# Rank scatter through a Pool ring: ring of four groups, direct rows in pairs of tiles, and an extra Pool drain

## Chip, cores, metric

One core of one Trainium2 chip. The metric is the device time of one execution in microseconds (us); medians of several executions are compared. The kernels of one job ran on one chip; the jobs ran on different chips (8, 1, 9 and 1), so runs of different jobs are compared by their ratio to the kernel before, which ran in every job.

## The reference

```
x: 8 x 2048 x 2560 float32, scores: 8 x 2048
ranks = argsort(argsort(scores, axis=1), axis=1)
out[b, ranks[b, n], :] = x[b, n, :]
```

Every row of 10 KB is moved to the place that its score's rank gives it: 168 MB read and 168 MB written.

## The kernel before

VectorE counts for every score how many others are smaller, which gives the rank. The rows are moved in two ways. Most go through SBUF: Pool loads a group (two tiles of 128 rows, 2.6 MB) into one of eight buffers and later scatters it with two indirect transfers. The rows of a few tiles ("direct") go from HBM to HBM, one transfer for each row, cut in 16 pieces of 640 B, issued by SyncE and ScalarE.

```
GROUPS = [(0, 1, range(B)), (P, 1, range(3))] + [(256 * i, 2, ()) for i in range(1, 8)]
#         (first row, tiles in the group, batches in which it goes direct)
ORDER = [2, 0, 1, 3, 4, 5, 6, 7, 8]
BULK = [(b, g) for b in range(B) for g in ORDER if b not in GROUPS[g][2]]
NBUF = 8
LAG = 2
...
with tc.tile_critical(no_gpsimd_drain=True):
    ...
    # SyncE and ScalarE in turn, for each direct row:
    line.eng.dma_start(
        out=out_bytes[bass.ds(at[i], ROW)], in_=x_bytes[b, row, :],
    ).then_inc(s_rows[line], 16)
    ...
    for k in range(1, NBUF):                      # Pool
        load(pl, k, s_load[k])
    for k, (b, g) in enumerate(BULK):
        i = k % NBUF
        if k >= LAG and k + NBUF - LAG < len(BULK):
            scatters_done(pl, k - LAG)            # wait: the group LAG back has landed
            load(pl, k + NBUF - LAG, s_load[(k - LAG) % NBUF])
        ...                                       # wait for load k and for the ranks
        for j in range(GROUPS[g][1]):
            scatter(k, j, 0, P, rank_i, s_scat[i][j])
    for k in range(max(0, len(BULK) - NBUF), len(BULK)):
        scatters_done(sp, k)                      # SyncE: the last waits
```

Pool's transfers run first in, first out on 16 DMA engines ("Pool's ring" below; in the profile before, all 177 landed in the order in which they were issued). A transfer has landed when its semaphore has its 16 increments. Pool's drain is an instruction at which, as e13 to e15 show, Pool waits until its transfers have landed; what more it costs is a subject of this study. LAG is how many groups may be scattered and not yet landed. With 11 direct tiles there are 61 groups, five of them of one tile ("half groups").

## Time and profile before

| | before |
|---|---|
| median of the runs | 794.83 us (794.64 to 796.62) |
| span of the profiled run | 795.4 us |
| transfers issued by Pool | 60 loads, 117 scatters |
| last scatter landed / last direct row landed | 791.3 / 727.6 us |
| Pool's drain at the very end | 3.02 us, from 791.64 |

The profiled execution was one of the slower ones (797.09 us of device time): the span is 1.6 to 2.1 us below the device time in all runs, so a run of the median should have its last landing near 789 us (an estimate). What bounds the kernel, and the lines that show it, are in the prediction.

### The profile page before, as it was taken

The page shows a single profiled execution, that of the slowest core. Times are in us where ns is not written, and L with a number is a line of the kernel's source. Part 1 is how long each engine was busy: PE and PEld are TensorE (multiplying, and loading weights), DVE is VectorE, ACT ScalarE, POOL GpSimd, SP SyncE. Part 2 cuts the span into 40 slices and gives each one's busy share as a digit, 9 for nine tenths or more (in the row PEclk, how much of TensorE's full clock was granted, in tenths as well). Part 3 has the DMA queues.
Part 4 walks back from the last instruction along what each step waited for, and adds up shares of the span by engine and source line. Part 5 has one row for each costly group of instructions (what it writes and reads, how often), then busy time and mean ns, then how long its engine had stood idle before and what let it go on. Part 6 is the DMA issues. An engine that isn't in the chain of part 4 may idle for free.

```text
span 795.4 us, 4586 instructions
## 1 busy us (share of the span) xinstructions
PE 33.3 (4%) x155; PEld 27.2 (3%) x155; DVE 411.2 (52%) x1002; POOL 148.4 (19%) x186
## 2 busy tenths in 40 slices
PE   3002010020020100200000000000000000000000
PEld 3001010010010100100000000000000000000000
DVE  6999999999999999999994000000000000000000
POOL 3102121212121212022111212122121212111600
PEclk9555555555555555555555555555555555555555
DMA  8999999999999999999999999999999999999994
GB/s 364 431 402 365 424 415 425 417 422 417 425 417 418 347 420 422 422 367 420 421 420 423 397 397 421 420 419 380 420 411 423 420 386 407 401 431 426 390 428 193
DMA packets 70737, 321.57 MB, mean 404 GB/s; under 512 B 25384, under 2 KB 47912, under 8 KB 47912
## 3 DMA queue, kind: packets, MB, share of 16 engines
q0 software_dynamic: 25488, 304.10, 91.3%
q1 hardware_dynamic: 22688, 9.94, 4.9%
q10 hardware_dynamic: 22528, 7.25, 3.9%
q14 instruction: 32, 0.26, 0.1%
q8 instruction: 1, 0.02, 0.0%
HBM read 167.84 MB, written 167.77 MB: 422 GB/s over the span
## 4 chain that ended last, share of the span: by engine, by line
DVE 47%; DMA 40%; issue 4%; POOL 3%; PE 1%; POOLq 0%; SPq 0%
DVE trash L258 41%; DMA out_dram<-x,rank_i 38%; DVE s_all L235 2%; DMA x<-in_x_dram 2%; POOL out_dram L361 2%; DVE rank L284 1%; DVE rank L290 1%; DVE rank_i L307 1%; POOL x L122 1%; DMA s_in<-in_scores_dram 0%; PE ps_all L190 0%; PE ps_col L169 0%; DVE rows_i L220 0%; POOLq L28 0%; DVE s_col L177 0%
## 5 line engine op out<-in xcount | busy, mean ns | idle before, releaser
L258 DVE TENSOR_SCALAR_CACHE_REDUCE trash<-s_all,s_col 128x1792 bf16<-128x1792 f32 (+9 forms) x248 | 315.3, 1306 | 0.3
L122 POOL DMA_DIRECT2D x<-in_x_dram x60 | 33.8, 565 | 545.8 <-DMA out_dram<-x,rank_i 376.5
L361 POOL DMA_INDIRECT out_dram<-x,rank_i x117 | 112.8, 964 | 59.0 <-issue 35.3
L258 DVE SCALAR_TENSOR_TENSOR trash<-s_all,s_col,mask 128x256 bf16<-128x256 f32 (+1 forms) x128 | 59.0, 461 | 0.0
L190 PE MATMUL ps_all<-ident,s_col 128*128 128x128 f32 x128 | 27.2, 399 | 247.4 <-DVE s_all L235 247.0
L190 PEld LDWEIGHTS ps_all<-ident,s_col 128*128 128x128 f32 x128 | 24.4, 213 | 249.4 <-DVE s_all L235 249.0
L235 DVE COPY s_all<-ps_all 128x512 f32<-128x512 f32 x32 | 20.1, 683 | 1.8 <-PE ps_all L190 1.5
L258 DVE DVE_READ_ACCUMULATOR trash<-s_all,s_col 128x1 f32 x248 | 19.9, 80 | 0.0
L290 DVE TENSOR_TENSOR rank<-rank,acc 128x2 f32<-128x2 f32 (+1 forms) x72 | 11.5, 160 | 2.5
L284 DVE TENSOR_TENSOR rank<-acc,acc 128x2 f32<-128x2 f32 (+1 forms) x72 | 11.5, 160 | 2.5
L307 DVE CAST rank_i<-rank 128x2 int32<-128x2 f32 (+1 forms) x61 | 10.7, 176 | 1.8
L258 DVE DVE_READ_ACCUMULATOR trash<-s_all,s_col,mask 128x1 f32 x128 | 10.2, 80 | 0.0
L300 PE MATMUL ps_row<-ident,rank 128*1 128x128 f32 x11 | 4.1, 372 | 101.3 <-DVE rank L290 92.7
L300 PEld LDWEIGHTS ps_row<-ident,rank 128*1 128x1 f32 x11 | 0.9, 79 | 105.0 <-DVE rank L290 95.5
L220 DVE TENSOR_SCALAR rows_i<-ps_row 1x128 int32<-1x128 f32 x11 | 3.0, 272 | 0.0
L177 DVE COPY s_col<-ps_col 128x128 f32<-128x128 f32 x1 | 0.3, 292 | 4.8 <-PE ps_col L169 4.8
L169 PE MATMUL ps_col<-ident,s_in 8*128 8x8 f32 x16 | 2.0, 261 | 4.0 <-DMA s_in<-in_scores_dram 4.0
L169 PEld LDWEIGHTS ps_col<-ident,s_in 8*128 8x128 f32 x16 | 1.9, 211 | 4.0 <-DMA s_in<-in_scores_dram 4.0
L150 POOL TENSOR_SCALAR_AFFINE_SELECT mask<-mask 128x256 f32<-128x256 f32 x2 | 0.8, 398 | 0.0
L162 DVE MEMSET acc<- 128x128 f32 x1 | 0.2, 165 | 1.1 <-SPq L98 1.1
L133 POOL MEMSET mask<- 128x512 f32 x1 | 0.5, 525 | 0.0
L132 POOL MEMSET ident<- 128x128 f32 x1 | 0.2, 204 | 0.5 <-SPq L98 0.5
(5 smaller groups left out, 0.7 us busy)
## 6 DMA issues: line engine op xcount, KB each, us to landing
x<-in_x_dram POOLq DMA_DIRECT2D x55, 2560.0 KB, 19.2
out_dram<-in_x_dram SPq DMA_DIRECT2D x704, 10.0 KB
out_dram<-in_x_dram ACTq DMA_DIRECT2D x704, 10.0 KB
x<-in_x_dram POOLq DMA_DIRECT2D x5, 1280.0 KB, 16.7
x<-in_x_dram SPq DMA_DIRECT2D x1, 2560.0 KB, 13.4
out_dram<-x,rank_i POOLq DMA_INDIRECT x117, 23.5
s_in<-in_scores_dram SPq DMA_DIRECT2D x1, 64.0 KB
```

Source lines behind the costliest of these rows:

```text
L122: line.eng.dma_start(out=xb[k % NBUF][:, :m * D], in_=x[b, r:r + P * m, :].rearrange("(p j) d -> p (j d)", j=m),).then_inc(sem, 16)
L150: nc.gpsimd.affine_select(out=part, in_=part, pattern=[[0, MMAX], [-1, P]], compare_op=OP.is_ge, fill=0.0, base=-half, channel_multiplier=1,)
L169: nc.tensor.transpose(out=ps_col[:, B * c:B * (c + 1)], in_=s_in[:, r + j:r + m * P:m], identity=ident[:B, :B],)
L190: nc.tensor.transpose(out=ps_all[:, P * c:P * (c + 1)], in_=s_col[:, c, b:b + 1].to_broadcast([P, P]), identity=ident[:],)
L220: nc.vector.tensor_scalar(out=rows_i[DIRECT.index((b, g))][:m, :], in0=ps_row[:m, :P], scalar1=float(b * N), scalar2=float(ROW), op0=OP.ad ...
L235: nc.vector.tensor_copy(out=s_all[:, 512 * q:512 * (q + 1)], in_=ps_all[:, 512 * q:512 * (q + 1)],)
L258: how.pop("do")(out=trash[i][:, :P * (hi_c - lo_c)], in0=s_all[:, P * lo_c:P * hi_c], accum_out=acc[which][:, col:col + 1], **how,)
L284: nc.vector.tensor_tensor(out=rank[:, cols], in0=acc[0][:, cols], in1=acc[1][:, cols], op=OP.add)
L290: nc.vector.tensor_tensor(out=rank[:, cols], in0=rank[:, cols], in1=acc[2][:, cols], op=OP.add)
L300: nc.tensor.transpose(out=ps_row[:m, :P], in_=rank[:, cols], identity=ident[:])
L307: nc.vector.tensor_copy(out=rank_i[:, cols], in_=rank[:, cols])
L361: nc.gpsimd.indirect_dma_start(out=out_flat, out_offset=bass.IndirectOffsetOnAxis(ap=index[:hi - lo, col:col + 1], axis=0), in_=xb[k % NBU ...
```

## The change

Its intent: a deeper ring, so that Pool's queue does not run dry; direct rows in pairs, so that no half group remains and one more tile goes direct; and Pool's drain, which the kernel pays after its last wait, moved beside the last waits.

```
-    GROUPS = [(0, 1, range(B)), (P, 1, range(3))] + [(256 * i, 2, ()) for i in range(1, 8)]
-    ORDER = [2, 0, 1, 3, 4, 5, 6, 7, 8]
+    GROUPS = [(0, 2, range(6))] + [(256 * i, 2, ()) for i in range(1, 8)]
+    ORDER = range(8)
...
-    LAG = 2
+    LAG = 4
...
-    with tc.tile_critical(no_gpsimd_drain=True):
+    with tc.tile_critical():
```

## The prediction

> **What bounds the kernel now.** I read the page in the order share of busy time, slices, queues, chain, then looked closer at single stretches.
>
> ```profile
> span 795.4 us, 4586 instructions
> ...
> DVE  6999999999999999999994000000000000000000
> ...
> DMA  8999999999999999999999999999999999999994
> GB/s 364 431 402 365 424 415 425 417 422 417 425 417 418 347 420 422 422 367 420 421 420 423 397 397 421 420 419 380 420 411 423 420 386 407 401 431 426 390 428 193
> ...
> q0 software_dynamic: 25488, 304.10, 91.3%
> q1 hardware_dynamic: 22688, 9.94, 4.9%
> q10 hardware_dynamic: 22528, 7.25, 3.9%
> ...
> HBM read 167.84 MB, written 167.77 MB: 422 GB/s over the span
> ```
>
> The DMA row is full from the first slice to the last. VectorE, which counts the ranks, is done by slice 22 (about 427 us) and is never far enough behind to matter after the start. The queue shares (q0 is Pool's, q1 and q10 are those of SyncE and ScalarE) add to 100% of 16 DMA engines' span, so there is no hole to fill by issuing earlier. But the GB/s row dips from 420 to 347 and 390 in places, with the busy row still full. The chain of waits puts the first half on VectorE ("DVE trash L258 41%"); I distrust that, since VectorE never pauses there and so every wait seems to end at one of its events. From 388 us on the chain is DMA only. Stretches around two dips, and a quiet one:
>
> ```profile
> core 0: us, PE busy (x) PEld busy (x) DVE busy (x) POOL busy (x), PEclk, DMA share, GB/s
> ...
> 64.00:66.00 2.00, 2.00 (x11) 2.00 (x10) 2.00 (x7) 1.39 (x3) 0.50 1.03 416
> 66.00:68.00 2.00, 0.50 (x3) 0.10 (x1) 2.00 (x3) 0.84 (x1) 0.71 1.06 344
> 68.00:72.00 4.00, 0.00 (x0) 0.00 (x0) 3.83 (x14) 1.27 (x2) 0.82 1.09 240
> ...
> 100.00:160.00 60.00, 4.30 (x18) 3.43 (x18) 58.99 (x144) 12.42 (x15) 0.53 1.02 419
> ...
> 266.00:270.00 4.00, 0.00 (x0) 0.00 (x0) 3.86 (x11) 0.00 (x0) 0.50 1.07 241
> ...
> 784.00:792.00 8.00, 0.00 (x0) 0.00 (x0) 0.00 (x0) 0.00 (x0) 0.50 0.07 29
> ```
>
> The packet records show what a dip is. In 66 to 68 us SyncE's queue started 116 packets of 640 B where it starts 38 to 47 in 2 us otherwise, while Pool's queue started 52 of its large ones instead of 76: Pool's ring had run dry on most engines, which spent the time on direct rows. Loads in a dip take up to 2.2 us instead of 0.76. Ring dry means: the wait for the scatter two groups back ended too late. Pool's own order of time at the first dip:
>
> ```profile
> 31.32 0.95 POOL L361 DMA_INDIRECT out_dram<-x,rank_i  x1 [0.30 <-issue]
> 63.73 0.57 POOL L122 DMA_DIRECT2D x<-in_x_dram  x1 [31.46 <-DMA out_dram<-x,rank_i]
> ```
>
> At 63.73 only the second group's scatter was still queued; the load issued there started its first packet at 67.8, four us later. Later dips (266, 344, 448, 548, 650 us) come where a one-tile group passes, which fills half of a ring slot.
>
> The semaphore arrivals in the trace (each transfer counts 16, one per engine) show the other half. In 90 to 160 us the last engine lands 4 to 4.7 us after the first; later the spread grows to 7 to 9 us and stays, and in the last 40 us fifteen engines are within 1.1 us while one lands 6.1 us after the next. So one engine trails, and it ends the kernel: last arrival 791.28 us, the others about 785. Where it trails, its step (one load, two scatters) takes about 13.4 us, that of the first engine 13.05.
>
> **The Trainium skill.** "DMA: Bandwidth & Descriptors", section "Queues, rings and completion order": each DMA engine goes round-robin between queue rows that have work. The trace agrees and is sharper than the page's packets of many descriptors: in 89 to 229 us SyncE's queue ran 2317 packets of 640 B, each with a 4 B one, against 4117 large Pool packets and their 4 B ones (27 turns per 24), so 1.00 of its packets per Pool turn. The same page, "Latency and other measured facts", says that engines 7 and 15 are usually slower; the trace shows one that trails, not its number. "HBM Reference", "Specifications (TRN2)": a core alone measures about 425 GB/s, bounded by its DMA engines; the quiet stretches show 419 to 429, so no ring depth gets past that.
>
> **The change part by part.**
> Packet times (medians of the records): load 20480 B 0.761 us, scatter 10240 B 0.385, direct piece 640 B 0.032, semaphore 4 B 0.009.
>
> (a) One more direct tile (12, not 11). A tile through SBUF costs each engine 4 x 0.761 + 8 x 0.385 = 6.12 us; a direct one 128 x (0.032 + 0.009) = 5.25. Gain 0.9 us on every engine.
>
> (b) Pairs. All groups are now two tiles (58 groups instead of 61, of which 5 were halves), so no half-filled slot. This removes the cause of the later dips.
>
> (c) Ring of four. After the wait for group k-4 three load-and-scatter pairs are still queued, not one: about 37 us of work on each engine (3 x 12.3) instead of 12.3. A 7 to 9 us spread plus the 4 us from issue to first packet ate the old 12.3; it cannot eat 37. Also four scatters go out at the start without a wait, so the dip at 66 us goes.
> What this is worth: not the excess on all engines (loads above 0.761 us add up to 13.4 us per engine, direct pieces 5.2), but what the trailing engine loses, because that one ends the kernel and at no time had an empty ring in the steady part. From its arrivals: at the start a load that needs 6.2 us landed 10.4 after the transfer before it, lost about 4 us; at 280 us 8.2 instead of 6.3, lost 1.9; at 459, 687 and 751 us 0.4 to 0.7 each. Some of that is direct rows done early, which are then not due later. I choose 6 us.
>
> (d) The drain. After the last wait at 791.28 us the instruction records have a Pool drain of 3.02 us at the very end, then two of 0.07 and 0.05. The intent is to run it beside SyncE's waits. But in the built program the new Pool drain waits for the same tick of SyncE that the other engines' drains wait for, and SyncE gives it after its last wait. So the 3.02 us moves a few instructions earlier, and the one after it becomes short. Gain 0; I put +0.3 for a handshake that now waits for it.
>
> (e) VectorE loses some counting work and takes the direct group first; the first direct rank is still ready at about 23 us, as now. Worth 0.
>
> Sum: 794.85 - 0.9 - 6 + 0.3 = 788.2; I say 788.5.
>
> **Rivals.**
> 1. The trailing engine alone counts and lost nothing that it did not use for direct rows: only (a) and (d), 794. For it: its ring was full in the steady part. Against it: the 10.4 us load.
> 2. Engine time counts on average: all 18.6 us of excess go, and with them part of the 6 us tail, 772 to 776. For it: the GB/s dips. Against it: the dips fall on the fifteen that wait for the trailing one anyway, and a deeper ring lets them run further ahead, not the one behind.
> 3. Direct rows become the end. Per queue 768 rows of two packets need 1536 turns. Pool's queue has 58 x 27 - 9 = 1557 turns (the first load goes by SyncE), of which some 20 are gone when rows start at 24 us: 1537. That is a tie. Before, dips gave about 33 turns for free and rows were issued out by 690 us. If turns are lost, what is left after Pool is dry runs at the issue rate, about 0.7 us a row (16 x 0.55 us and 1.7 us for the indices). I expect at most a few rows, since SyncE is some 20 rows ahead; 20 rows late would be 14 us, 802.
> 4. Fifteen engines that never wait load HBM all the time and slow the sixteenth: nothing in the quiet stretches speaks for more than its present 13.4 us.
>
> **Range and chances.** Rival 1 sets the upper side, with a few us for rival 3; a part of rival 2 sets the lower. 781 to 796. Faster by over 2% needs under 779: 0.06. Slower by over 2% needs over 811: 0.03. Within: 0.91.
>
> **What would show it.** Right: no slice with 640 B surges and under 400 GB/s between 60 and 700 us; loads all near 0.76 us; a spread between first and last engine that grows past 9 us, because nothing holds the fifteen back; a last arrival at about 784 us; a Pool drain of about 3 us still after it; direct rows issued until 740 us or later. Wrong: a last arrival at 775 or less (rival 2), SyncE still issuing rows when Pool's scatters have all landed (rival 3), or the 3 us drain before the last wait (step d).

## The result, and the profile after

The changed kernel took 799.91 us (median of 4, 799.4 to 800.62), the kernel before 794.83: a ratio of 1.006, interval 1.0042 to 1.0077. Ratios here and below are the mean time of one kernel's fast runs over that of the other's of the same rounds, so not quite the ratio of the medians. It is slower by 5 us, where 6 us less was forecast.

The page of the changed kernel, with the rows that answer to those of before:

```profile
span 798.0 us, 4795 instructions
...
DMA  8999999999999999999999999999999999999930
GB/s 369 426 400 415 426 415 424 419 421 421 418 422 419 420 420 424 417 426 416 424 415 422 418 424 418 426 414 424 421 418 422 420 420 421 423 418 419 410 145 13
...
q0 software_dynamic: 24912, 301.48, 88.8%
q1 hardware_dynamic: 24736, 10.60, 4.8%
q10 hardware_dynamic: 24576, 7.91, 4.0%
```

The dips are gone: no slice between the fourth and the one before the last full one is under 410 GB/s. But the last two slices hold little (145 and 13 GB/s, where the kernel before has 428 and 193), though the span is longer. The same kernel in stretches (the last two columns are the mean busy share of the 16 DMA engines, and GB/s):

```profile
62.00:72.00 10.00, 3.56 (x17) 3.13 (x17) 9.89 (x18) 3.79 (x5) 0.67 1.03 418
262.00:270.00 8.00, 0.22 (x1) 0.22 (x2) 7.83 (x18) 1.22 (x2) 0.50 1.03 427
...
770.00:789.00 19.00, 0.00 (x0) 0.00 (x0) 0.00 (x0) 0.00 (x0) 0.50 0.06 25
789.00:798.00 9.00, 0.00 (x0) 0.00 (x0) 0.00 (x0) 0.00 (x0) 0.50 0.00 0
```

The same stretches before, for the dips:

```profile
62.00:72.00 10.00, 3.67 (x16) 3.27 (x16) 9.79 (x24) 3.77 (x5) 0.67 1.05 329
262.00:270.00 8.00, 0.00 (x0) 0.00 (x0) 7.76 (x24) 2.39 (x3) 0.50 1.08 282
```

The deeper ring did to the dips what it was meant to do: 329 and 282 GB/s became 418 and 427. And from 770 to 789 us the busy share is 0.06, which is one engine of 16. Fifteen engines were done by 770, and the sixteenth went on alone to 788.8 us. The whole gain of the fifteen is lying there unused.

The second thing is in the 9 us after 789, where no DMA engine is busy. SyncE's waits, before and then after:

```profile
SPq L28 <- DMA out_dram<-x,rank_i: 100.3, 8, 79.2
...
SPq L420 <- PEq L420: 3.3, 2, 2.9
```

```profile
SPq L28 <- DMA out_dram<-x,rank_i: 23.1, 7, 3.7
...
SPq L98 <- POOLq L98: 6.6, 1, 6.6
...
SPq L98 <- DMA out_dram<-in_x_dram: 1.3, 1, 1.3
```

Columns: us in total, number of waits, longest. The wait of 6.6 us is a wait for Pool at the end of the section: Pool's new drain, 6.85 us from 790.36. Before, the drain stood at the very end and took 3.02 us; SyncE's share of it is the 2.9 us that the profile puts down to another engine that had long been done. The 1.3 us are a wait for the last direct rows, which now end after the last scatter (790.2 against 788.8 us). SyncE issued its last direct row at 764.8 us, before at 690.2.

### The profile page after: what moved, and what is told of

The parts are those of the page before. It is cut to its first block, busy times and chain, and to the rows that moved or that the text cites. A ratio compares the mean times of both kernels' runs of the same rounds, so it can differ in the third digit from the quotient of the medians.

```text
span 798.0 us, 4795 instructions
## 1 busy us (share of the span) xinstructions
PE 30.9 (4%) x150; PEld 26.8 (3%) x150; DVE 409.0 (51%) x962; POOL 145.6 (18%) x182
## 4 chain that ended last, share of the span: by engine, by line
DVE 50%; another core or an unknown queue 22%; DMA 12%; POOL 6%; issue 4%; PE 1%; POOLq 0%; SPq 0%
DVE trash L258 43%; DMA out_dram<-x,rank_i 6%; DMA x<-in_x_dram 6%; POOL out_dram L361 5%; DVE s_all L235 2%; POOL x L122 1%; DVE rank L284 1%; DVE rank L290 1%; DVE rank_i L307 1%; PE ps_all L190 0%; DMA s_in<-in_scores_dram 0%; PE ps_col L169 0%; DVE rows_i L220 0%; POOLq L28 0%
## 5 line engine op out<-in xcount | busy, mean ns | idle before, releaser
L258 DVE TENSOR_SCALAR_CACHE_REDUCE trash<-s_all,s_col 128x1792 bf16<-128x1792 f32 (+7 forms) x240 | 314.4, 1345 | 0.3
L122 POOL DMA_DIRECT2D x<-in_x_dram x57 | 32.1, 565 | 510.4 <-DMA out_dram<-x,rank_i 344.1
L258 DVE SCALAR_TENSOR_TENSOR trash<-s_all,s_col,mask 128x256 bf16<-128x256 f32 x128 | 61.4, 480 | 0.0
L284 DVE TENSOR_TENSOR rank<-acc,acc 128x2 f32<-128x2 f32 x64 | 10.3, 161 | 2.2
L290 DVE TENSOR_TENSOR rank<-rank,acc 128x2 f32<-128x2 f32 x64 | 10.3, 161 | 2.2
L307 DVE CAST rank_i<-rank 128x2 int32<-128x2 f32 x58 | 10.1, 174 | 1.8
L258 DVE DVE_READ_ACCUMULATOR trash<-s_all,s_col,mask 128x1 f32 x128 | 10.4, 82 | 0.0
L300 PE MATMUL ps_row<-ident,rank 128*2 128x128 f32 x6 | 1.8, 304 | 15.2 <-DVE rank L290 15.2
L220 DVE TENSOR_SCALAR rows_i<-ps_row 2x128 int32<-2x128 f32 x6 | 1.6, 272 | 0.0
```

The costliest lines, as they stand in the source:

```text
L122: line.eng.dma_start(out=xb[k % NBUF][:, :m * D], in_=x[b, r:r + P * m, :].rearrange("(p j) d -> p (j d)", j=m),).then_inc(sem, 16)
L220: nc.vector.tensor_scalar(out=rows_i[DIRECT.index((b, g))][:m, :], in0=ps_row[:m, :P], scalar1=float(b * N), scalar2=float(ROW), op0=OP.ad ...
L258: how.pop("do")(out=trash[i][:, :P * (hi_c - lo_c)], in0=s_all[:, P * lo_c:P * hi_c], accum_out=acc[which][:, col:col + 1], **how,)
L284: nc.vector.tensor_tensor(out=rank[:, cols], in0=acc[0][:, cols], in1=acc[1][:, cols], op=OP.add)
L290: nc.vector.tensor_tensor(out=rank[:, cols], in0=rank[:, cols], in1=acc[2][:, cols], op=OP.add)
L300: nc.tensor.transpose(out=ps_row[:m, :P], in_=rank[:, cols], identity=ident[:])
```

## The experiments

Fifteen kernels were run. "Last scatter" and "last row" are when the last scatter and the last direct row landed, "drain" is the first of Pool's drains after the last landing, in the profiled run, all in us. "One look" is a single execution. The kernel before was timed again in each job: medians 794.54 (e1 to e4), 795.13 (e5 to e8), 795.5 (e9 to e12), 795.57 (e13 to e15).

| run | Pool transfers | last scatter | last row | drain | median | ratio to before (interval) |
|---|---|---|---|---|---|---|
| before | 177 | 791.3 | 727.6 | 3.02 | 794.83 | |
| after | 173 | 788.8 | 790.3 | 6.85 | 799.91 | 1.0060 (1.0042 to 1.0077) |
| e1 change without the moved drain | 173 | 787.6 | 788.9 | 6.85 | 798.70 | 1.0050 (1.0037 to 1.0062) |
| e2 only the moved drain | 177 | 789.1 | 729.2 | 3.01 | 794.50 | 0.9995 (0.9983 to 1.0008) |
| e3 only the ring of four | 177 | 787.8 | 725.5 | 3.18 | 793.61 | 0.9985 (0.9972 to 0.9998) |
| e4 only the pairs | 173 | 787.4 | 788.6 | 6.85 | 798.35 | 1.0045 (1.0032 to 1.0058) |
| e5 the change again | 173 | 788.8 | 790.2 | 6.85 | 799.84 | 1.0054 (1.0042 to 1.0066) |
| e6 e1 and four tiny loads | 177 | 789.9 | 789.7 | 6.28 | 799.63 | 1.0054 (1.0041 to 1.0067) |
| e7 no direct rows, ring of four | 191 | 793.7 | | 8.32 | 804.39 | 1.0113 (1.0100 to 1.0126) |
| e8 no direct rows, ring of two | 191 | 811.5 (slow) | | 8.32 | 805.8 (fast runs) | 1.0129 (1.0112 to 1.0147) |
| e9 e3 with 12 direct tiles | 175 | 788.8 | 785.2 | 8.73 | 800.41 | 1.0062 (1.0049 to 1.0076) |
| e10 e1 with 10 direct tiles | 176 | 788.3 | 673.7 | 7.09 | 798.05 | 1.0034 (1.0020 to 1.0049) |
| e11 e3 and four tiny loads | 181 | 790.3 | 724.2 | 3.18 | 796.32 (one look) | |
| e12 e1, five loads cut in two | 178 | 788.1 | 784.6 | 6.44 | 797.96 | 1.0030 (1.0015 to 1.0045) |
| e13 e1 with an early drain | 173 | 788.5 | 789.8 | 0.05 | 794.65 | 0.9988 (0.9973 to 1.0002) |
| e14 e3 with an early drain | 177 | 788.2 | 726.0 | 0.05 | 792.87 | 0.9964 (0.9950 to 0.9979) |
| e15 e1 with a drain half way | 173 | 802.6 | 777.5 | 4.15 | 809.75 (one look) | |

### First job: the change taken apart

e1, the change with the old place of the drain:

```
-    with tc.tile_critical():
+    with tc.tile_critical(no_gpsimd_drain=True):
```

> The changed kernel with the drain as it was before (only at the very end). After the change Pool's drain took 6.85 us where it took 3.02 before, both after the last scatter had landed (790.15 and 791.28 us). Theory A, the new place of the drain makes it longer: here one drain of about 3.0 us at the end, time 796 us, 4 us less than the changed kernel's 799.9. Theory B, the drain is longer because of what stands in Pool's ring (depth 4 or the pairs), wherever it stands: a drain of about 6.8 us at the end, time 799.5 to 800.

The drain took 6.85 us at the very end. Theory A falls; where the drain stands does not make it longer. The time, 798.70, is 0.8 us under what theory B said.

e2, the kernel before with the opposite edit:

> The kernel before with only the drain moved. Theory A (place): drain 6.8 us, time 798.6 us. Theory B (what stands in the ring): drain 3.0 us, only moved ahead of the end, time 794.8 to 795.3 us.

Drain 3.01 us at the end of the section; the ratio to before is 0.9995. Moving it is worth nothing, as the prediction's step (d) said, and costs nothing.

e3, the kernel before with `LAG = 4` in place of `LAG = 2`:

> The kernel before with only the ring of four (11 direct tiles, half groups stay). Theory B with depth as the cause: final drain near 6.8 us. In both theories the dips at 66 us and at the half groups go, fifteen engines run ahead and one ends the kernel 15 us or more after them, with a last arrival of 787 to 791 us: what I predicted as a gain of 6 us was lost time of the fifteen, not of the one that ends the kernel (then 790 or 791). If the gain was real, the last arrival is at 785.

The drain stayed at 3.18 us, so the depth of the ring is not its cause. The dips went, and the last scatter landed at 787.8 us where e2's landed at 789.1. The ring of four is worth 1.2 us (0.15%; by the interval 0.2 to 2.2 us), not 6. This kernel in stretches:

```profile
60.00:72.00 12.00, 3.30 (x16) 3.06 (x16) 11.72 (x28) 3.94 (x5) 0.64 1.02 414
...
760.00:765.00 5.00, 0.00 (x0) 0.00 (x0) 0.00 (x0) 0.00 (x0) 0.50 1.00 416
765.00:785.00 20.00, 0.00 (x0) 0.00 (x0) 0.00 (x0) 0.00 (x0) 0.50 0.12 50
```

The dip at 66 us is gone (414 GB/s), and what was gained is again a stretch at the end in which few engines, at last one, are busy (0.12 of 16 from 765 to 785 us).

e4, the kernel before with the new GROUPS and ORDER alone:

> The kernel before with only the pairs of tiles (12 direct tiles, ring of two, no early drain). If the pairs themselves removed the later dips: no stretch under 400 GB/s after 100 us. Last arrival 788 to 792 us; the last engine ends it here too, 7 to 9 us behind the others because a ring of two holds them back. Theory B with the depth as the cause: drain 3.0 us, time 793 to 796. With the longer life of the direct rows as the cause (they are issued until the end): drain 6.8 us, time 797 to 800.

Drain 6.85 us, time 798.35: the whole loss comes with the pairs. It is the drain's: e4 is 3.81 us slower than the kernel before of its job, and the drain is 3.83 us longer than before. The second forecast of the entry held in its figure, but not for the reason that it gives (see e10). This kernel's GB/s row, and SyncE's wait in which the drain lies (again put down to another engine that had long been done):

```profile
GB/s 363 433 403 363 425 416 424 416 424 416 424 416 425 415 422 416 416 413 408 416 411 401 418 418 420 416 388 419 419 414 420 408 413 403 414 414 411 422 390 18
...
SPq L420 <- PEq L420: 7.1, 2, 6.7
```

The prediction's step (b), that pairs remove the later dips, held in part: with a ring of two the row still has 388, 401 and 403 in it after the start, where before it had 347, 367 and 380. The last engine ended 10.5 us after the next one, not 7 to 9.

### Second job: what makes one engine slow, and the drain

In the packet records of all kernels above one engine stands out. In a quiet stretch (100 to 250 us of the changed kernel) 2820 of 2995 scatter packets took exactly 385 ns. Most of the rest (138) took 390 to 440, one after the other at a distance of about 0.44 us, up to 16 in each group, as many as one engine has: I read them as the packets of one engine, whose scatters are about 7% slower. Over a run, packets of 390 to 500 ns number 587 to 770, and their time over 385 ns adds up to 13.6 to 17.5 us. (In e3, e11 and e14 they include 70 to 100 of a short burst on many engines near 760 us, after the direct rows; its cause is not known.) In the kernel before they stop between 700 and 710 us, soon after the last direct row was issued (690) and before the last one landed (727); in the changed kernel they go on to 767 us (last issue 764.8).

e5, the changed kernel once more:

> The changed kernel beside the others of this job. 799.5 to 800 us, drain 6.85 us, last scatter 788.8 and last direct row about 1.3 us after it, as in its first profile.

As expected.

e6, e1 with four loads of 2 KB each on Pool behind its first loads:

```
+        for i in range(4):
+            nc.gpsimd.dma_start(
+                out=spare[:, 4 * i:4 * i + 4], in_=x[0, 0:P, 4 * i:4 * i + 4]
+            ).then_inc(s_spare, 16)
```

> The changed kernel with the drain at the end and four more, tiny loads on Pool (128 x 16 B each), so that Pool issues 177 transfers as the kernel before does, where the changed one issues 173. So far the drain took 3.01 to 3.18 us in the three kernels with 177 and 6.85 us in the three with 173, whatever the depth of the ring. Theory C, the drain works off something that depends on the number of Pool's transfers: drain about 3.0 us, time 795 us. Theory D, it is long because direct rows are issued until the end: drain 6.85 us, time 799 us.

Neither: the drain was 6.28 us. It does move with Pool's transfers, but not with their plain number. The last scatter came 2.3 us later than in e1, and 1.1 us later than in e5 of its own job, for which I have no explanation.

e7, no direct rows:

```
-    GROUPS = [(0, 2, range(6))] + [(256 * i, 2, ()) for i in range(1, 8)]
+    GROUPS = [(256 * i, 2, ()) for i in range(8)]
```

> All 128 tiles through SBUF in 64 pairs, no direct rows, ring of four, drain at the end. In all six kernels so far one engine has its scatter packets at about 410 ns instead of 385, some 600 to 700 of them, 14 to 18 us in all, and that stops soon after the direct rows are all issued. Theory E, issuing direct rows slows that engine: no such packets here, all engines within 4 us of each other at the end. Work per engine 64 x 8 x 0.7575 + 128 x 8 x 0.3815 = 778.5 us plus 3.5 at the start, last arrival 783 to 787, and 787 to 790 if the instruction fetches stay on one engine; time 788 to 796 depending on the drain. Rival F, that engine is slow anyway: 1024 scatter packets of 410 ns, last arrival 808 to 812, time over 814. For theory D the drain is 3.0 us here; for C it can be anything, with 191 transfers.

Only 52 scatter packets over 390 ns were left, 0.7 us in all. That the slow engine goes with the direct rows is shown; rival F falls. So does theory D, with a drain of 8.32 us. By which path they reach it (their issue, or the transfers that carry the issue) is not. The page of this kernel:

```profile
DMA  9999999999999999999999999999999999999991
GB/s 369 430 403 436 415 426 429 421 428 422 426 429 427 430 433 429 429 430 429 434 427 430 431 433 428 430 431 431 432 429 428 435 427 429 434 428 430 428 430 71
```

It moves 430 GB/s to the last full slice, but it has 14 MB more than the kernel before to move through the engines, and ends later: the last scatter at 793.7 us, the time 804.4, both outside the forecast. The forecast of engines within 4 us was wrong: the spread grew to 9.7 us at 416 us and stayed there. Growth ended when VectorE did (424 us), and about when the 8 KB reads of the instruction queue did: nine of 0.31 us each between 32 and 433 us, 2.8 us in all, too little for it. I leave that spread open.

e8, the same with a ring of two:

> The same with a ring of two. If all engines are even, 12.2 us of queued work is more than the spread plus the four us of a new issue, and the time is that of the ring of four within 1 us. If it is 2 us or more slower, the ring depth has a worth of its own that the trailing engine hid.

Three of six runs were slow, the profiled one too, so its landing is not used. The fast ones were at 805.5 to 805.9 us, 1.4 us above e7's median: between the two forecasts, and the same small worth of the deeper ring as in e3.

### Third job: what sets the drain

e9, e3 with `(P, 1, range(4))` in place of `(P, 1, range(3))`:

> Twelve direct tiles as in the change, but of one tile each, so four half groups stay; ring of four, drain at the end; Pool issues 175 transfers, four of them half loads. Theory G, the drain is short where half loads are among Pool's transfers (3.01 to 3.18 us with five of them, 6.85 and 8.32 with none): about 3 us, at most 4.5; time about 794.5 to 796. Theory H, it goes with twelve direct tiles whose rows last to the end: 6.8 us, time 798.5. In both the direct rows end after the last scatter or within 1 us of it, since their 1536 turns per queue are as many as Pool's.

The drain was 8.73 us, with four half loads. Theory G falls, and H's 6.8 is not met either. The direct rows ended 3.6 us before the last scatter, which the forecast had excluded.

e10, e1 with `range(5)` in place of `range(6)`:

> Pairs, but five of them direct (10 tiles), ring of four, drain at the end; 176 transfers, no half loads. Direct rows are then issued out by about 640 to 660 us, long before the end. Theory G: drain 6.8 to 7.2 us, time 798 to 799. Theory H: drain near 3 us, time 794 to 795. Last arrival 788.5 to 790, as each direct tile less costs every engine 1.75 us and gives 1.4 us back on the slow one.

Direct rows had all landed at 673.7 us, and the drain was 7.09 us. Theory H falls. Note that three transfers more than in e1 made 0.245 us more, 82 ns each; e7's 18 more made 1.476 us, again 82 ns each.

e11, e3 with the four tiny loads of e6:

> The ring-of-four-only kernel (drain 3.18 us) with four tiny loads more on Pool. With the changed kernel they took the drain from 6.85 to 6.28 us. If each transfer counts in the drain by its own size or kind, it moves here by a similar half us, to 2.6 or 3.7. Only the drain is looked at.

3.18 us, as without them. Together with e6 this says that a transfer early in the program need not count.

e12, e1 with the first five of Pool's loads cut in two:

```
+            if k < 6:
+                ...
+                nc.gpsimd.dma_start(out=xb[k][:, :D], in_=src[:, :D]).then_inc(s_load[k], 16)
+                nc.gpsimd.dma_start(out=xb[k][:, D:2 * D], in_=src[:, D:2 * D]).then_inc(s_half[k], 16)
```

> The changed kernel (drain at the end) with five of Pool's first loads cut into two half loads each (178 transfers, 10 of them of 10240 B a row). Everything after the first 50 us is as in the changed kernel. Theory G: drain 3 to 4.5 us, time 795 to 796.5. If it stays above 6 us, half loads are not the cause and what sets the drain stays open.

6.44 us: half loads are not the cause.

### Fourth job: can a drain be paid early?

e13, e1 with a drain behind Pool's last scatter; e14, the same in e3; e15, e1 with a drain before group 40:

```
+        nc.gpsimd.drain()

         for k in range(max(0, len(BULK) - NBUF), len(BULK)):
             scatters_done(sp, k)
```

> The changed kernel with a Pool drain right after Pool's last scatter is issued (about 757 us), where it really runs beside SyncE's last waits; no new drain at the section's end. Theory I, a drain is work of Pool's own on transfers already issued, about 82 ns each, done once: the early one takes some 7 us or waits for the transfers until 789, the one at the end 0.1 us; time 792 to 793, 6 to 7 us less than the changed kernel. Theory J, the cost comes at the end whatever was drained before: a last drain of 6.8 us, time 798.5.

> The ring-of-four-only kernel (793.6 us, drain 3.18 us at the end) with the same early drain. Theory I: time 790.3 to 791, the fastest so far. Theory J: 793.6.

> The changed kernel with a Pool drain in the middle (before group 40), where 123 of its 173 transfers have been issued; only the drains are looked at. Theory I in the form that a drain counts transfers since the last time that Pool cleared its list, 82 ns each: the middle one shows some of the cost, the last one covers 50 transfers, 4.1 to 4.3 us instead of 6.85. If the last one stays 6.85, it does not count transfers since a drain.

Theory I holds in its main point. The early drain ran from 754.3 to 791.9 us in e13 and from 757.8 to 789.8 in e14, and the one at the end then took 0.05 us. It is not free: it ended 1.6 us (e14) and 2.1 us (e13) after the last landing, because a drain also waits for the transfers. SyncE's waits in e14:

```profile
SPq L28 <- DMA out_dram<-x,rank_i: 97.5, 8, 76.5
...
SPq L98 <- POOLq L98: 1.2, 1, 1.2
```

The 6.6 us wait for Pool of the changed kernel is 1.2 us here. e13, where that wait is 2.0 us, has a ratio to before of 0.9988, where the changed kernel had 1.0054 (e5) and 1.0060: some 5 us faster, and no slower than before. e14 is the fastest kernel, 0.36% faster than before. Both are about 2 us short of the forecast.

In e15 the drain in the middle waited for everything in flight (54.6 us) and the kernel was slow (809.75 us in one look). But its last drain is what counts: 50 transfers were issued after the middle one, and the last took 4.145 us, which is 50 x 82 + 45 ns. So this drain cost about 82 ns for each transfer issued since the drain before it; the forecast of 4.1 to 4.3 us was made with that rule. That Pool also clears a list of transfers at other moments is inferred, not shown. Read that way, the changed kernel's 6.847 us are 83 transfers, and the kernel before's 3.015 are 36: its list was cleared after transfer 141 of 177, the changed kernel's after transfer 90 of 173. e7, e10 and e1 agree on 90. The kernels with half groups do not come out whole (36.2 for before, 38.2 for e3, 105.9 for e9), so there the rule is rough. What clears the list without a drain is open, and with it why the pairs made the drain longer. The four runs with the change's transfers and no early drain have 6.847 us to the nanosecond, with a ring of two or of four; with the transfers of the kernel before, the ring of four moved it from 3.01 to 3.18.

## Why the prediction was wrong

**What bounds the kernel: right.** The DMA engines, with one that trails and ends the kernel. Of the signs that were named, these came: no surges of 640 B packets, a spread that grew past 9 us (to 25.3 at the last scatter, 763.5 to 788.8 us), loads near 0.76 us (mean 0.764, before 0.790), direct rows issued until after 740 us. These did not: a last arrival at 784 us (it was 788.8, and 790.3 for the direct rows), and a drain of about 3 us. The ceiling that the prediction named, 419 to 429 GB/s, was a little low: without direct rows (e7) every full slice from the 12th on moved 427 to 435.

**Step (c), the worth of the ring, 6 us: wrong, and this is the step where the mechanism failed.** The prediction took the last arrival of each transfer for the arrivals of one engine. They are not. The slow scatter packets let that engine be followed by itself. In the kernel before its scatters of one group ended at about 97 us, when the last engine landed them at 99.6; it became the last one at about 160 us. So the load at 80 us that "landed 10.4 after the transfer before it" was late on other engines: the slow engine had begun the scatters behind it at 78.0 us. At 280 us the same: the slow engine's next scatters began at 277.7 us, so its load had landed by then, and the 280.2 was another engine's. Those delays hit engines that had time to lose. Measured alone (e3), the ring is worth 1.2 us. The prediction had written the right test beside it, "what the trailing engine loses, because that one ends the kernel", and then applied it to the wrong engine. Rival 1, "the trailing engine alone counts and lost nothing", was nearer the truth for this term. Rival 2 falls: the excess of the loads went, and 1.2 us at most were won by it (e3). Of rival 4 nothing is seen: from 100 to 250 us the scatter packets of 390 to 500 ns took 410.5 ns on average before and 409.4 after.

**Step (d), the drain, +0.3 us: right about its place, wrong about its length.** It does stand after the last wait. But I took its 3.02 us for a constant. It depends on Pool's transfers, which the pairs changed (how, is open): 6.85 us, so the term is +3.8 us and not +0.3. e4 shows it: with the pairs alone the drain has the full 6.85. e13 shows that it is what costs the time: with the drain issued early, the loss is gone.

**Step (b), no half groups, no dips: right in part.** With a ring of two the later dips became smaller (lowest slice 388 GB/s in e4 where it was 347); with a ring of four they go though half groups are there (e3).

**Step (a), one more direct tile, -0.9 us: not seen.** The last scatter of e4 came 1.7 us before that of e2, but its last direct row landed at 788.6, so 0.5 us are left of it in these two profiles, and nothing by the medians (e4's 3.81 us are all the drain's).

**Rival 3, the direct rows become the end: came true in small.** The count of turns said a tie; the rows ended 1.1 to 1.5 us after the last scatter in the changed kernel, e1, e4, e5 and e13. In e6 and e12, which have six pairs direct too, they ended 0.2 and 3.4 us before it.

**The sum, corrected:** 794.5 (the kernel before in e4's job) + 3.8 (drain) = 798.3, and e4 measured 798.35. The ring of four, worth 1.2 us alone, gave nothing more on top of the pairs (e1 798.70): there the direct rows end the kernel. The changed kernel itself was at 799.9 and in e5 at 799.84, 1.2 us above e1, but in other jobs. Against the kernel before of its own job it is 1.0060 and 1.0054, where e1 is 1.0050, and the intervals overlap: the difference is not clear of noise. Its profiles do have later landings (790.3 and 790.2 us, e1's 788.9), and why stays open.

## What to carry to other kernels

When transfers are bound by the engine that ends last, follow that engine, and not the latest arrival at each moment, which belongs to now one and now another; here a fuller queue mostly let the others wait at the end instead of in between. Look at what a kernel does after its last landing, too: a drain that had been 3 us became 7 by a change of the transfers alone, and a drain issued right after the last transfer paid it beside the traffic (e13, e14), all but about 2 us. And a change of three parts is best measured as three: here the part that looked most harmless cost it all.

## What the Trainium skill lacked or had wrong

- No page has what a Pool drain costs. The runs show 82 ns for each transfer on Pool since an earlier drain plus 45 ns (e15: 50 transfers, 4.145 us), 3.01 to 8.73 us in kernels without an earlier drain, and that it waits for the transfers in flight (54.6 us in the middle of e15).
- "DMA: Bandwidth & Descriptors", "Latency and other measured facts", gives SWDGE descriptor rings as the best guess for slower engines 7 and 15. Here one engine (its number is not in the trace) has scatter packets of about 410 ns instead of 385, in some 590 to 770 packets a run, but only in kernels in which SyncE and ScalarE issue direct rows; with Pool's traffic alone (e7) 52 packets are of 390 to 500 ns, though the engines still spread by 9.7 us there. That this is engine 7 or 15 is not shown.
- The same page, "Queues, rings and completion order", has an engine drain a whole packet of about 9 to 17 descriptors before it turns to the next queue. Here it turned after every record: one 640 B or 4 B record of each other queue for each record of Pool's, 1.00 by count.
